# Moving the activation sums behind the next pair's additions, and three smaller moves, in a hybrid decoder layer

## The chip, the core and the metric

The kernel runs on one core of one Trainium2 chip. The metric is device time in microseconds from one execution of the whole program; lower is better. TensorE (PE) multiplies, VectorE (DVE), ScalarE (ACT) and GpSimd (POOL) do element-wise work, and SyncE (SP) as well as ACT issue DMA transfers. Each engine takes its own instructions strictly in the order in which they were built, and semaphores make it wait for others.

## What is computed

One layer of a decoder trunk on 1024 tokens of width 1024, in float32. Three branches read a normalised, projected x; then a ConvFFN is added.

```python
x += (sum_b sigmoid(G_b) * (branch_b @ W_br[b])) @ W_out     # RWKV-7, stick-breaking attention, memory attention
x += conv_ffn(x)

def memory_branch(q, mem, mem_g, w_kv, q_g, k_g):            # 256 memory tokens, 4 heads x 128
    kv = rms_norm(mem, mem_g) @ w_kv
    mk, mv = jnp.split(kv, 2, axis=-1)
    ...
def conv_ffn(x, g, w_up, conv_w, conv_b, w_down):            # D_FF = 2816
    h = rms_norm(x, g) @ w_up
    hp = jnp.pad(h, ((0, 0), (CONV_W - 1, 0), (0, 0)))
    acc = conv_b + hp[:, 0:t] * conv_w[0]
    for i in range(1, CONV_W):
        acc = acc + hp[:, i:i + t] * conv_w[i]
    gate, val = jnp.split(acc, 2, axis=-1)
    return (jax.nn.silu(gate) * val) @ w_down
```

## The kernel before

**Products.** A float32 product is made of three fast ones: each operand is split into a high part (a rounded copy, made by ACT) and a low part (the rest, made by DVE or POOL), and PE adds high x high, high x low and low x high. `split_w` does that for a weight: L83 makes `wh` on ACT, L86 or L89 makes `wl` on DVE or POOL.

**First half.** A long list of small items (projections, gates, key and query work, memory keys) is woven between the steps of the attention loops. Much of the order is left to a scheduler. Two helpers restrict it: `pinned` keeps an instruction in program order among those marked so, and `behind(ins, prev)` puts `ins` after `prev`. `last_fin` is the last copy of a finished PSUM bank that some item left behind. The attention of a head pair goes through `front` (L979, ACT), `weigh` (a scan on DVE, L985), `mid` (transposes on PE, copied by ACT at L997) and `back` (products of the tiles `at` with the values `A`). The keys of a head pair are split in `k_split` (L928, L929 on ACT, then L930, L931 on DVE). L936 copies a finished projection out of its bank, L937 squares it. The memory keys are made in `mk`, one head per call; L1119 and L1120 write the square and the scaled key of each head into two tiles `st["k"]`. Tiles come from `t4(tag)`: the tag names a ring of buffers, "w4" with 3 (the default) and "at" with 7. An instruction that takes a buffer waits for the last reader of what lay there, a DMA too.

**Up phase.** `up_phase` multiplies with W_up in blocks of two by two: seven products of 512-wide halves instead of eight, which needs sums of weights before and sums of activations behind. `pairs` lists 22 column pairs n = 0 to 21: even n are gate columns, odd n the value columns of the same block f = n // 2. `step(n, i)` issues product i of pair n; for n > 2 the order is 1, 5, 6, 2, 7, 4, 3. Each product is 12 matmuls. What DVE does with the banks: L1685 adds product 6's bank to `p1`, and the bank is then used again by product 7, which accumulates in it; L1698 and L1699 (behind product 7), L1708 (behind 4), L1717 (behind 3). `conv_half` makes the convolution of one half: L1627 on ACT, L1629 and L1630 on DVE; for even n a sigmoid `sg` on ACT (L1632); then the product of gate and value on DVE (L1635) into a tile `gall` (or `ga`, block 1). `prep1` to `prep3` make the next pair's weight sums on POOL (L1572, L1576, L1582, L1583) and split weights (L1554 on ACT, L1555 on POOL). `act_sums(f, late)` adds, when both halves of block f are there, the activation quarters (L1646, two additions for `late=False`, two for `late=True`) and stores them in DRAM (L1654, L1661, L1662, DMAs issued by ACT).

**Down phase.** `down_phase` goes through seven stages i of 11 blocks f. `prep` loads three blocks ahead and splits them: L1846 on DVE (some weights are differences), L1851 and L1852 on ACT, L1853 on DVE (`da`), L1854 on POOL (`dw`). At a stage's end `drain` takes the banks; `complete(tt)` then adds a finished output tile to the residual (L1874) in the next stage, `release` issues the stores. `last_residual` (L1915, L1916) adds the residual into `keep` late in stage 4.

Of the kernel before, what the change touches and what calls it, by code (L numbers as in the profile page):

```python
# [15 lines left out]
AF = mybir.ActivationFunctionType  # L16
# [34 lines left out]
class Trunk:  # L51
# [847 lines left out]
    def sb_qk(self, p, out):  # L899
        nc = self.nc  # L900
        st = {}
        lo64, hi64 = slice(0, 64), slice(64, 128)

        def k_fin(pp):
            kr, sq = self.t4(), self.t4()
            for h in range(2):
                self.leave(nc.scalar.activation(kr[:, h * 512 : (h + 1) * 512], pp[h], AF.Copy))
            nc.scalar.activation(sq, kr, AF.Square)
            st["k"] = sq, kr

        def k_ss():
            st["ex"] = self.expand_heads(self.head_norm(self.head_ss(st["k"][0]), 2, SBD, 1.0))

        def k_bc():
            kr = st["k"][1]
            bc = self.bcast_heads(st["ex"])
            for h in range(2):
                hs = slice(h * 512, (h + 1) * 512)
                nc.vector.scalar_tensor_tensor(kr[:, hs], kr[:, hs], self.par("sbk"), bc[h], ALU.mult, ALU.mult)
            st["K"] = [], []  # L920

        def k_split(i):
            kr = st["k"][1]
            K, KL = st["K"]
            for x in (K, KL):
                x.append(self.t4("qk", F32R))
            q, o = (lo64, hi64) if i == 0 else (hi64, lo64)
            nc.scalar.activation(K[i][q], kr[q], AF.Copy)  # L928
            nc.scalar.activation(K[i][o], kr[q], AF.Copy)  # L929
            nc.vector.tensor_tensor(KL[i][q], kr[q], K[i][q].bitcast(F32), ALU.subtract)  # L930
            nc.vector.tensor_tensor(KL[i][o], kr[q], K[i][q].bitcast(F32), ALU.subtract)  # L931

        def q_fin(pp):
            qr, sq = self.t4(), self.t4()
            for h in range(2):
                self.leave(nc.scalar.activation(qr[:, h * 512 : (h + 1) * 512], pp[h], AF.Copy))  # L936
            nc.scalar.activation(sq, qr, AF.Square)  # L937
            st["q"] = sq, qr

        def q_split(i):  # L940
            qr = st["q"][1]
            st.setdefault("S", []).append(self.t4("qk", F32R))
            S = st["S"][i]
            q, o = (lo64, hi64) if i == 0 else (hi64, lo64)
            g = self.par("sbq")[q]
            nc.scalar.activation(S[q], qr[q], AF.Copy, scale=g)
            nc.vector.scalar_tensor_tensor(S[o], qr[q], g, S[q].bitcast(F32), ALU.mult, ALU.subtract)
            if i == 1:
                out.extend((st["S"], *st["K"], st["f"]))

        def q_ss():
            nf = self.small("nf", [128, 16])
            st["f"] = self.head_norm(self.head_ss(st["q"][0]), 2, SBD, SBD ** -0.5, nf)

        w = self.I["w_in"]
        hooks = {1: lambda: k_split(1), 3: q_ss, 4: lambda: q_split(0), 6: lambda: q_split(1)}
        kq = {4: k_bc, 5: lambda: k_split(0)} if p else {5: k_bc, 6: lambda: k_split(0)}
        kh = {} if p else {k: functools.partial(self.difference, k - 3) for k in (3, 4, 5, 6)}
        return self.proj_item(w[18 + p], k_fin, kh), k_ss, self.proj_item(w[14 + p], q_fin, kq), hooks
# [82 lines left out]
    def mem_kv(self):  # L1042
        nc = self.nc
        mhi, mlo, sqs, st = [], [], [], {}
# [61 lines left out]
        def mk(h):  # L1106
            w = self.split_w(self.I["w_mk"][h])
            yield
            if h == 0:
                st["k"] = self.t4(), self.t4()  # L1110
            sq, kr = st["k"]
            hs = slice(h * 256, (h + 1) * 256)
            pk = self.ps("mm")[:, :256]
            for k in range(8):
                ks = slice(k * 128, (k + 1) * 128)
                self.mm3([pk], [a[:, ks] for a in w], [[mx(t, k, slice(0, 256))] for t in (mhi, mlo)], k == 0, k == 7)
                if k == 3:
                    yield
            nc.scalar.activation(sq[:, hs], pk, AF.Square)  # L1119
            nc.scalar.activation(kr[:, hs], pk, AF.Copy, scale=self.par("memk"))  # L1120
            self.mk = sq, kr, *st["r"]
            yield
# [394 lines left out]
    def up_phase(self, raws, t2, operand, high, low, late, sums):  # L1517
        nc = self.nc
# [19 lines left out]
        W, st = {}, {}  # L1538
# [125 lines left out]
        def step(n, i):  # L1664
# [15 lines left out]
            elif i == 6:  # L1680
# [2 lines left out]
                if (n, "u1") not in st:  # L1683
                    st[n, "u1"] = u_tile()
                self.pinned(nc.vector.tensor_tensor(st[n, "u1"][:, R2], Bk, st[n, "p1"], ALU.add))  # L1685
                if n > 2 and pairs[n - 1][2]:
                    act_sums(pairs[n - 1][1], True)
            elif i == 7:
                Bk = st.pop((n, "B"))
                product(n, 7, Bk, False, True)  # L1690
# [9 lines left out]
            elif i == 40:  # L1700
                Dk = st[n, "D"] = bank()
                product(n, 4, Dk, True, True)
            elif i in (4, 41):
                if i == 4:
                    step(n, 40)
                Dk = st.pop((n, "D"))
                v = st[n, "u2"]
                nc.vector.tensor_tensor(v[:, L2], v[:, L2], Dk, ALU.subtract)  # L1708
                if n == 0:
                    return st.pop((n, "u2"))  # L1710
                if n + 1 < len(pairs):
                    conv(n, 1, st.pop((n, "u2")))
            elif i == 3:
                C = st.pop((n, "C"))
                product(n, 3, C, False, True)
                u = st.pop((n, "u1"))
                nc.vector.tensor_tensor(u[:, R2], C, u[:, R2], ALU.add)  # L1717
                if n == 0:
                    return u
                if n + 1 == len(pairs):  # L1720
                    conv(n, 1, st.pop((n, "u2")))
                if n == 1:
                    return u
                conv(n, 0, u)
                if n + 1 == len(pairs):
                    self.last_sums = [functools.partial(act_sums, pairs[n][1], late) for late in (False, True)]
                elif pairs[n][2]:
                    act_sums(pairs[n][1], False)

        def u1_first(n):  # L1730
            A = st.pop((n, "A"))
# [48 lines left out]
        for n in range(1, len(pairs)):  # L1780
# [3 lines left out]
            for i in order:  # L1784
# [4 lines left out]
                if n == 1 and i == 4:  # L1789
                    step(2, 1)  # L1790
                elif n == 2 and i == 6:
                    conv(1, 0, u)
                elif n == 3 and i in (5, 6, 7, 4):
                    late, part = ((False, 0), (False, 1), (True, 0), (True, 1))[(5, 6, 7, 4).index(i)]
                    act_sums(0, late, (part,))
                if n == 1 and i == 6:
                    prep3(1)
                    prep1(2)
# [15 lines left out]
    def down_phase(self):  # L1814
        nc = self.nc
# [108 lines left out]
        for s, (i, f) in enumerate(steps):  # L1924
# [10 lines left out]
                t_sums(s // 2)  # L1935
            if s + ahead < len(steps):
                prep(s + ahead)
            if f < 4:
                complete(f)
            elif f == 5:  # L1940
                release()
            if s in (2, 4):
                self.last_sums.pop(0)()
# [184 lines left out]
```

## Time and profile before

| | us |
|---|---|
| median of 3 runs (lowest to highest) | 1789.28 (1788.69 to 1789.63) |
| profiled execution | 1788.33 |
| its span | 1786.6 |
| busy PE, DVE, ACT, POOL | 1774.7, 1185.1, 883.3, 698.3 |
| one up-phase pair (seven products) | 19.04 |

The granted clock was 1.000. In the views times are microseconds from the span's start; a timeline row has start, busy time, engine, line, operation, out<-in, shape and count, and in brackets the idle time ahead of it with what ended it. A group of equal neighbours stands in one row (x2, x3). In the list of waits a row reads: engine line waited for: us in total, times, longest. Lines are those of the kernel before; in the changed one, lines behind L1685 are two lower (four lower from L1727 to L1790).

### The profile page before, as it was taken

The numbers are of one execution on the slowest core, as the hardware profiler recorded it, in microseconds if no ns is written. First come the engines' busy times: TensorE is split into PE (matmuls) and PEld (weight loads), VectorE is DVE, ScalarE is ACT, GpSimd is POOL, SyncE is SP. The second block draws the span as 40 slices with busy tenths as digits, with TensorE's granted clock in tenths as the row PEclk, the third lists the DMA queues.
The fourth block names the chain that finished last, engine by engine and source line by source line (L and its number), as shares of the span: only waits on it lengthen the run. The fifth ranks groups of instructions, "written<-read, shape, count | busy, mean of one in ns | idle before, by whom it ended". The sixth has DMA issues, their size and how long they took to land.

```text
span 1786.6 us, 27452 instructions
## 1 busy us (share of the span) xinstructions
PE 1774.7 (99%) x10481; PEld 1442.4 (81%) x10481; DVE 1185.1 (66%) x1687; ACT 883.3 (49%) x1667; POOL 698.3 (39%) x409
## 2 busy tenths in 40 slices
PE   9999999999999999999999999999999999999999
PEld 7777778878888888787777888887888888888887
DVE  5666674787888655243533873698767777795597
ACT  6544344566566635444546434454444445445343
POOL 1233252222231012122433321257777677535454
PEclk9999999999999999999999999999999999999999
DMA  4256574111112333658763653323323333396475
GB/s 185 74 166 193 181 244 148 51 57 42 54 57 77 103 126 93 203 181 278 269 228 145 230 211 105 108 89 124 101 89 104 115 104 113 109 329 224 142 246 202
DMA packets 120757, 263.39 MB, mean 147 GB/s; under 512 B 28329, under 2 KB 41129, under 8 KB 120498
## 3 DMA queue, kind: packets, MB, share of 16 engines
q1 hardware_dynamic: 82434, 193.31, 33.1%
q10 hardware_dynamic: 34416, 55.72, 8.5%
q0 software_dynamic: 3776, 12.62, 2.3%
q8 instruction: 82, 1.34, 0.3%
q14 instruction: 49, 0.40, 0.1%
HBM read 180.04 MB, written 81.53 MB: 146 GB/s over the span
## 4 chain that ended last, share of the span: by engine, by line
PE 61%; issue 1%; DVE 1%; POOL 1%; ACT 1%; DMA 1%; ACTq 0%; DVEq 0%; POOLq 0%; SPq 0%
PE mm L139 53%; PE g L139 8%; PE g L122 1%; POOL dw L1854 1%; DMA vmd<-w 0%; ACT wh L83 0%; DMA qk<-vd 0%; DVE qk L715 0%; ACT w L885 0%; DVE gall L1646 0%; DVE w L886 0%; DVE ga L1635 0%; DVE keep L1874 0%; DVE g L1629 0%; DVE g L1630 0%
## 5 line engine op out<-in xcount | busy, mean ns | idle before, releaser
L89 POOL TENSOR_TENSOR wl<-wr,wh 128x1024 fp32r<-128x1024 f32 x58 | 147.8, 2550 | 368.2 <-ACT wh L83 355.0
L139 PE MATMUL mm<-xhi,wh 128*128 128x512 f32 x784 | 260.5, 413 | 1.4 <-ACT xhi L222 1.0
L139 PE MATMUL mm<-xlo,wh 128*128 128x512 f32 x784 | 243.6, 392 | 0.1
L139 PE MATMUL mm<-xhi,wl 128*128 128x512 f32 x784 | 242.2, 390 | 0.0
L139 PEld LDWEIGHTS mm<-xlo,wh 128*128 128x128 f32 x784 | 147.0, 188 | 33.4 <-DVE xlo L225 1.0
L139 PEld LDWEIGHTS mm<-xhi,wl 128*128 128x128 f32 x784 | 147.2, 188 | 32.7
L139 PEld LDWEIGHTS mm<-xhi,wh 128*128 128x128 f32 x784 | 136.6, 189 | 31.1 <-issue 7.9
L139 PE MATMUL mm<-dw,da 128*128 128x512 f32 x528 | 120.9, 390 | 0.0
L83 ACT ACTIVATE wh<-wr 128x1024 fp32r<-128x1024 f32 x75 | 79.5, 1060 | 81.5 <-PE mm L139 57.2
L139 PE MATMUL mm<-BT,l 128*128 128x512 f32 x504 | 117.9, 389 | 0.3 <-POOL l L1555 0.3
L139 PEld LDWEIGHTS mm<-dw,da 128*128 128x128 f32 x528 | 98.9, 188 | 21.3 <-DVE da L1853 0.8
L1854 POOL TENSOR_TENSOR dw<-draw,dw 128x512 fp32r<-128x512 f32 x55 | 83.6, 1530 | 76.1 <-ACT dw L1852 74.2
L985 DVE TENSOR_TENSOR_SCAN at<-at,at 128x128 f32<-128x128 f32 (+3 forms) x64 | 91.0, 1428 | 33.1 <-ACT at L979 33.0
L139 PEld LDWEIGHTS mm<-BT,l 128*128 128x128 f32 x504 | 94.5, 188 | 20.3 <-POOL l L1555 0.7
L139 PE MATMUL mm<-BT,wh 128*128 128x512 f32 x352 | 108.6, 390 | 1.7 <-DVE u L1685 1.7
L139 PE MATMUL mm<-B,wh 128*128 128x512 f32 x352 | 108.6, 389 | 0.0
L195 POOL TENSOR_TENSOR hf<-rs,half 128x16 f32<-128x16 f32 (+1 forms) x18 | 49.2, 2734 | 142.2 <-DVE rs L192 137.8
L1853 DVE TENSOR_TENSOR da<-draw,da 128x512 fp32r<-128x512 f32 x77 | 66.9, 877 | 49.1 <-ACT da L1851 48.8
L139 PE MATMUL g<-dw,da 128*128 128x512 f32 x396 | 90.6, 389 | 0.4 <-POOL dw L1854 0.4
L1851 ACT ACTIVATE da<-draw 128x512 fp32r<-128x512 f32 x77 | 48.3, 628 | 80.7 <-PE mm L139 29.9
L139 PEld LDWEIGHTS g<-dw,da 128*128 128x128 f32 x396 | 74.2, 188 | 16.2 <-POOL dw L1854 0.8
L1555 POOL TENSOR_TENSOR l<-it,l 128x1024 fp32r<-128x1024 f32 x20 | 48.0, 2402 | 85.5 <-ACT l L1554 85.5
(343 smaller groups left out, 3972.1 us busy)
## 6 DMA issues: line engine op xcount, KB each, us to landing
wr<-in_w_in_dram SPq DMA_DIRECT2D x49, 512.0 KB, 3.7
draw<-actd SPq DMA_DIRECT2D x77, 256.0 KB, 3.3
at<-scr SPq DMA_DIRECT2D x28, 512.0 KB, 5.6
draw<-in_w_down_dram SPq DMA_DIRECT2D x55, 256.0 KB, 4.8
rw<-in_w_up_dram SPq DMA_DIRECT2D x22, 512.0 KB, 3.6
actd<-gall ACTq DMA_DIRECT2D x41, 256.0 KB, 3.4
gsd<-w ACTq DMA_DIRECT2D x20, 512.0 KB, 2.7
wr<-in_w_up_dram SPq DMA_DIRECT2D x18, 512.0 KB, 3.6
```

The source lines that it names most:

```text
L83: ins = self.nc.scalar.activation(hi, raw, AF.Copy)
L89: self.last_wl = self.nc.gpsimd.tensor_tensor(lo, raw, hi.bitcast(F32), ALU.subtract)
L122: self.pinned(self.nc.tensor.transpose(out, in_, self.ident[:n, :n]))
L139: self.pinned(self.nc.tensor.matmul(*a, **k))
L195: nc.gpsimd.tensor_tensor(out, t[:, :n], self.half[:, :n], ALU.pow)
L985: self.pinned(nc.vector.tensor_tensor_scan(sn[:, :W][:, ::-1], sn[:, :W][:, ::-1], self.smask[:, 1024 - W :][:, ::-1], 1.0, ALU.mult, ALU. ...
L1555: self.last_low = keep(eng.tensor_tensor(lo, src, hi.bitcast(F32), ALU.subtract))
L1851: self.pinned(nc.scalar.activation(A[:, 0], a, AF.Copy))
L1853: self.pinned(nc.vector.tensor_tensor(A[:, 1], a, A[:, 0].bitcast(F32), ALU.subtract))
L1854: nc.gpsimd.tensor_tensor(Wt[:, 1], w, Wt[:, 0].bitcast(F32), ALU.subtract)
```

## The change

Four pieces.

1. In `k_split` both key copies on ACT are put behind `last_fin`.
2. The two memory-key tiles come from the ring "at" instead of "w4".
3. The activation sums of a block leave `step`. For odd pairs n - 1 > 2 they are now issued in pair n: the first two behind product 6's addition (L1685), the last two behind product 7's additions (L1699). Before, the first two stood at the end of pair n - 1, the last two behind L1685. Block 0's sums, spread over products 5, 6, 7 and 4 of pair 3, now stand at 5, 6, 6 and 7.
4. In stage 4 of the down phase the tiles are completed at blocks 0, 2, 4 and 6 instead of 0 to 3, and released at block 8 instead of 5.

```diff
@@ -925,8 +925,8 @@
             for x in (K, KL):
                 x.append(self.t4("qk", F32R))
             q, o = (lo64, hi64) if i == 0 else (hi64, lo64)
-            nc.scalar.activation(K[i][q], kr[q], AF.Copy)
-            nc.scalar.activation(K[i][o], kr[q], AF.Copy)
+            for x in (q, o):
+                self.behind(nc.scalar.activation(K[i][x], kr[q], AF.Copy), self.last_fin)
             nc.vector.tensor_tensor(KL[i][q], kr[q], K[i][q].bitcast(F32), ALU.subtract)
             nc.vector.tensor_tensor(KL[i][o], kr[q], K[i][q].bitcast(F32), ALU.subtract)
 
@@ -1107,7 +1107,7 @@
             w = self.split_w(self.I["w_mk"][h])
             yield
             if h == 0:
-                st["k"] = self.t4(), self.t4()
+                st["k"] = self.t4("at"), self.t4("at")
             sq, kr = st["k"]
             hs = slice(h * 256, (h + 1) * 256)
             pk = self.ps("mm")[:, :256]
@@ -1683,8 +1683,6 @@
                 if (n, "u1") not in st:
                     st[n, "u1"] = u_tile()
                 self.pinned(nc.vector.tensor_tensor(st[n, "u1"][:, R2], Bk, st[n, "p1"], ALU.add))
-                if n > 2 and pairs[n - 1][2]:
-                    act_sums(pairs[n - 1][1], True)
             elif i == 7:
                 Bk = st.pop((n, "B"))
                 product(n, 7, Bk, False, True)
@@ -1724,8 +1722,6 @@
                 conv(n, 0, u)
                 if n + 1 == len(pairs):
                     self.last_sums = [functools.partial(act_sums, pairs[n][1], late) for late in (False, True)]
-                elif pairs[n][2]:
-                    act_sums(pairs[n][1], False)
 
         def u1_first(n):
             A = st.pop((n, "A"))
@@ -1791,8 +1787,10 @@
                 elif n == 2 and i == 6:
                     conv(1, 0, u)
                 elif n == 3 and i in (5, 6, 7, 4):
-                    late, part = ((False, 0), (False, 1), (True, 0), (True, 1))[(5, 6, 7, 4).index(i)]
-                    act_sums(0, late, (part,))
+                    for late, part in {5: ((False, 0),), 6: ((False, 1), (True, 0)), 7: ((True, 1),)}.get(i, ()):
+                        act_sums(0, late, (part,))
+                elif n > 3 and n % 2 == 0 and i in (6, 7):
+                    act_sums(pairs[n - 1][1], i == 7)
                 if n == 1 and i == 6:
                     prep3(1)
                     prep1(2)
@@ -1935,9 +1933,11 @@
                 t_sums(s // 2)
             if s + ahead < len(steps):
                 prep(s + ahead)
-            if f < 4:
+            if i != 4 and f < 4:
                 complete(f)
-            elif f == 5:
+            elif i == 4 and f < 8 and f % 2 == 0:
+                complete(f // 2)
+            elif f == (8 if i == 4 else 5):
                 release()
             if s in (2, 4):
                 self.last_sums.pop(0)()
```

PE's order is the same in both. What moves elsewhere, at the places that the prediction speaks of:

ACT in head pair 1 of the attention, before. `qk_536` is the second split key tile of head pair 1, `w4_522` the projection that leaves its bank at L936, `at_534` a transposed attention tile that PE reads next.

```order
L928 ACTIVATE qk_536_3179<-w4_446_2750 64x1024
L979 ACTIVATE at_519_3114<-g_520_3115,nf_418_2590 128x512
L979 ACTIVATE at_519_3114<-g_521_3119,nf_418_2590 128x128
L929 ACTIVATE qk_536_3179<-w4_446_2750 64x1024
L936 ACTIVATE w4_522_3129<-mm_495_2977 128x512
L936 ACTIVATE w4_522_3129<-mm_496_2978 128x512
L83 ACTIVATE wh_527_3143<-wr_526_3141 128x1024
L937 ACTIVATE w4_523_3130<-w4_522_3129 128x1024
L997 ACTIVATE at_524_3134<-g_525_3135 128x384
L979 ACTIVATE at_531_3156<-g_532_3157,nf_418_2590 128x512
L979 ACTIVATE at_531_3156<-g_533_3161,nf_418_2590 128x256
L997 ACTIVATE at_534_3165<-g_535_3166 128x512
```

After:

```order
L979 ACTIVATE at_519_3114<-g_520_3115,nf_418_2590 128x512
L979 ACTIVATE at_519_3114<-g_521_3119,nf_418_2590 128x128
L936 ACTIVATE w4_522_3129<-mm_495_2977 128x512
L936 ACTIVATE w4_522_3129<-mm_496_2978 128x512
L83 ACTIVATE wh_527_3143<-wr_526_3141 128x1024
L937 ACTIVATE w4_523_3130<-w4_522_3129 128x1024
L997 ACTIVATE at_524_3134<-g_525_3135 128x384
L979 ACTIVATE at_531_3156<-g_532_3157,nf_418_2590 128x512
L979 ACTIVATE at_531_3156<-g_533_3161,nf_418_2590 128x256
L929 ACTIVATE qk_536_3179<-w4_446_2750 64x1024 x2
L997 ACTIVATE at_534_3165<-g_535_3166 128x512
L946 ACTIVATE qk_551_3264<-w4_522_3129,params_70 64x1024
```

The two copies of `qk_536` have gone from in front of the bank copies (L936) to the place between the second pair of L979 and the L997 that makes `at_534`.

POOL between pairs 3 and 4 of the up phase, before. `wl_1819` and `wl_1828` are low parts of pair 4's weights, `l4_1817` the low part of its weight sums, `it_1838` a sum for pair 5.

```order
L1555 TENSOR_TENSOR wl_1819_11338<-wr_1782_11128,wh_1818_11337 128x1024
L1555 TENSOR_TENSOR l4_1817_11321<-it_1815_11317,l4_1816_11320 128x1024
L1572 TENSOR_TENSOR it_1838_11476<-rw_1812_11294 128x512
L1576 TENSOR_TENSOR it_1838_11476<-it_1838_11476,rw_1811_11293 128x512
L1582 TENSOR_TENSOR rw_1812_11294<-rw_1811_11293,rw_1812_11294 128x512
L1555 TENSOR_TENSOR wl_1828_11417<-wr_1783_11129,wh_1827_11416 128x1024
```

After:

```order
L1555 TENSOR_TENSOR wl_1819_11339<-wr_1782_11128,wh_1818_11338 128x1024
L1555 TENSOR_TENSOR wl_1828_11412<-wr_1783_11129,wh_1827_11411 128x1024
L1555 TENSOR_TENSOR l4_1817_11322<-it_1815_11318,l4_1816_11321 128x1024
L1572 TENSOR_TENSOR it_1838_11472<-rw_1812_11294 128x512
L1576 TENSOR_TENSOR it_1838_11472<-it_1838_11472,rw_1811_11293 128x512
L1582 TENSOR_TENSOR rw_1812_11294<-rw_1811_11293,rw_1812_11294 128x512
```

The low part `wl_1828` has moved ahead of `l4_1817`, past the three sums.

DVE in pair 8 of the up phase, before; `u_1933` is written by L1685 and L1717, `u_1939` by L1698 to L1708.

```order
L1646 TENSOR_TENSOR gall_10748<-gall_10748 128x512 x2
L1618 MEMSET u_1933_12083 128x2
L1685 TENSOR_TENSOR u_1933_12083<-mm_1932_12070,p1_1928_12051 128x512
L1646 TENSOR_TENSOR gall_10748<-gall_10748 128x512 x2
L1618 MEMSET u_1939_12126 128x2
L1698 TENSOR_TENSOR u_1939_12126<-mm_1932_12070,p1_1928_12051 128x512
L1699 TENSOR_TENSOR u_1939_12126<-mm_1929_12053,u_1939_12126 128x512
L1708 TENSOR_TENSOR u_1939_12126<-u_1939_12126,mm_1940_12130 128x512
L1629 SCALAR_TENSOR_TENSOR g_1942_12145<-u_1939_12126,params_70,g_1942_12145 128x512
```

After (L1696, L1697, L1706 and L1715 are the old L1698, L1699, L1708 and L1717):

```order
L1618 MEMSET u_1933_12078 128x2
L1685 TENSOR_TENSOR u_1933_12078<-mm_1932_12065,p1_1928_12046 128x512
L1646 TENSOR_TENSOR gall_10748<-gall_10748 128x512 x2
L1618 MEMSET u_1939_12122 128x2
L1696 TENSOR_TENSOR u_1939_12122<-mm_1932_12065,p1_1928_12046 128x512
L1697 TENSOR_TENSOR u_1939_12122<-mm_1929_12048,u_1939_12122 128x512
L1646 TENSOR_TENSOR gall_10748<-gall_10748 128x512 x2
L1706 TENSOR_TENSOR u_1939_12122<-u_1939_12122,mm_1940_12130 128x512
L1715 TENSOR_TENSOR u_1933_12078<-mm_1929_12048,u_1933_12078 128x512
L1629 SCALAR_TENSOR_TENSOR g_1942_12145<-u_1939_12122,params_70,g_1942_12145 128x512
```

The two sums ahead of L1685 have gone behind it, the two behind it have gone behind the old L1699, and the old L1717 has come up ahead of the first L1629.

ACT at the end of pair 8 and the start of 9, before. `sg_1941` and `sg_1944` are the two sigmoid tiles, `l4_1960` the high part of pair 10's weight sums.

```order
L1627 ACTIVATE g_1942_12145<-u_1939_12126,params_70 128x512
L1627 ACTIVATE g_1943_12151<-u_1939_12126,params_70 128x512
L1627 ACTIVATE g_1945_12171<-u_1933_12083,params_70 128x512
L1554 ACTIVATE l4_1950_12190<-s4_1947_12183 128x512
L1632 ACTIVATE sg_1941_12144<-g_1942_12145 128x512
L1632 ACTIVATE sg_1941_12144<-g_1943_12151 128x512
L1669 ACTIVATE p1_1953_12207<-mm_1952_12194 128x512
L1627 ACTIVATE g_1946_12177<-u_1933_12083,params_70 128x512
L1632 ACTIVATE sg_1944_12170<-g_1945_12171 128x512
L1632 ACTIVATE sg_1944_12170<-g_1946_12177 128x512
L1554 ACTIVATE l4_1960_12245<-it_1959_12242 128x1024
```

After:

```order
L1627 ACTIVATE g_1942_12145<-u_1939_12122,params_70 128x512
L1627 ACTIVATE g_1943_12151<-u_1939_12122,params_70 128x512
L1627 ACTIVATE g_1945_12171<-u_1933_12078,params_70 128x512
L1627 ACTIVATE g_1946_12177<-u_1933_12078,params_70 128x512
L1554 ACTIVATE wh_1948_12186<-rw_1908_11916 128x1024
L1632 ACTIVATE sg_1941_12144<-g_1942_12145 128x512
L1632 ACTIVATE sg_1941_12144<-g_1943_12151 128x512
L1554 ACTIVATE l4_1950_12190<-s4_1947_12183 128x512
L1669 ACTIVATE p1_1953_12207<-mm_1952_12194 128x512
L1632 ACTIVATE sg_1944_12170<-g_1945_12171 128x512
L1554 ACTIVATE l4_1960_12245<-it_1959_12242 128x1024
L1632 ACTIVATE sg_1944_12170<-g_1946_12177 128x512
```

The second half's last sigmoid (from `g_1946`) now stands behind `l4_1960`; the copy of `wh_1948` has gone behind all four L1627.

## Prediction

> **What bounds the kernel now.** The page's part 1 comes first.
>
> ```profile
> PE 1774.7 (99%) x10481; PEld 1442.4 (81%) x10481; DVE 1185.1 (66%) x1687; ACT 883.3 (49%) x1667; POOL 698.3 (39%) x409
> ```
>
> TensorE is the bound: its 1774.7 us stand in a span of 1786.6, and the change leaves its instructions and their order alone. So the time can only move by stretches in which PE waits. The list of PE's waits has ten rows; these are the ones that the change can touch (total, times, longest, in us).
>
> ```profile
> PE mm L139 <- DVE u L1685: 1.7, 1, 1.7
> PE mm L139 <- DVE wl L86: 0.9, 2, 0.5
> PE mm L139 <- ACT w L936: 0.4, 1, 0.4
> PE g L139 <- POOL dw L1854: 0.4, 1, 0.4
> PE mm L139 <- POOL l L1555: 0.3, 1, 0.3
> ```
>
> Together they are 3.7 us, all single events. By the timeline around them PE also loses about 0.1 us after each while its pipeline refills. So at most some 4.2 us can be gained. What can be lost has no such cap, since the up phase runs the same pair of column blocks 22 times: a wait that the new order makes there comes back in each.
>
> **Key copies (sb_qk).** ACT's timeline in head pair 1, then PE's.
>
> ```profile
> 366.08 1.06 ACT L929 ACTIVATE qk<-w 64x1024 fp32r<-64x1024 f32 x1
> 367.04 1.05 ACT L936 ACTIVATE w<-mm 128x512 f32<-128x512 f32 x2
> ...
> 370.40 1.04 ACT L979 ACTIVATE at<-g,nf 128x512 f32<-128x512 f32 x2
> 371.33 0.60 ACT L997 ACTIVATE at<-g 128x512 f32<-128x512 f32 x1
> ```
>
> ```profile
> 367.67 0.50 PE L139 MATMUL mm<-xhi,wh 128*128 128x512 f32 x1 [0.42 <-ACT w L936]
> 372.93 1.09 PE L139 MATMUL mm<-at,A 128*64 128x128 f32 x14
> ```
>
> PE waits at 367.67 because a key copy (L929) runs ahead of the bank copies (L936). With both key copies behind, L936 starts about 0.5 us earlier (when PE has left the bank) and some 0.1 of the 0.42 stays: gain 0.3 and the refill, 0.4 in all. But the copies don't vanish. The built order puts them between the second L979 and the L997 at 371.33, and ACT runs from 367.04 on without a gap. That L997 then moves by -0.5 + 2 x 0.97 (1.06 less the overlap of neighbours) to about 372.75, ends near 373.35, and PE wants its tile from about 372.55 on (372.93 less the 0.4 gained). The first of the 14 matmuls reads an older tile. New wait 0.7, refill 0.1: the part loses 0.4. Ends: -0.5 (no matmul of the group needs the tile early) to +0.6. Head pairs 0, 2 and 3 already stood in the new order.
>
> **Memory keys (mem_kv).** ACT's timeline, then one PE row.
>
> ```profile
> 620.97 0.47 ACT L1120 ACTIVATE w<-mm,params 128x256 f32<-128x256 f32 x1 [2.44 <-DMA vmd<-w]
> 621.34 1.05 ACT L83 ACTIVATE wh<-wr 128x1024 fp32r<-128x1024 f32 x1
> 622.42 1.24 ACT L1020 ACTIVATE ys<-mm,jk 64x128 f32<-64x128 f32 x4
> ```
>
> ```profile
> 627.32 0.39 PE L139 MATMUL mm<-qk,wl 128*128 128x256 f32 x1 [0.49 <-DVE wl L86]
> ```
>
> L1120 waits 2.44 us for the store of the memory values, whose buffer it takes; the weight's high part (L83) stands behind it, and both wl waits (0.9) follow. In buffers of "at" this wait is gone. The first PE wait goes whole. At the second, the chain is 1.0 us earlier (it now waits for the L1020 copies, whose bank PE has just left) while PE wants it 0.5 earlier: 0.3 stays. Gain 1.0 with the refills; ends 0.5 and 1.2. The two "at" buffers taken are long read; nothing queues for them.
>
> **Sums at the start (pairs 3 and 4).** Rows of DVE, ACT, POOL and PE.
>
> ```profile
> 1216.25 1.77 DVE L1646 TENSOR_TENSOR gall<-gall 128x512 f32<-128x512 f32 x1
> 1238.91 0.68 DVE L1685 TENSOR_TENSOR u<-mm,p 128x512 f32<-128x512 f32 x1
> ```
>
> ```profile
> 1218.18 1.06 ACT L1554 ACTIVATE wh<-wr 128x1024 fp32r<-128x1024 f32 x1 [2.08 <-PE mm L139]
> ```
>
> ```profile
> 1219.32 2.41 POOL L1555 TENSOR_TENSOR wl<-wr,wh 128x1024 fp32r<-128x1024 f32 x1
> 1227.49 2.41 POOL L1555 TENSOR_TENSOR l<-it,l 128x1024 fp32r<-128x1024 f32 x1 [5.76 <-ACT l L1554]
> 1240.08 2.84 POOL L1555 TENSOR_TENSOR wl<-rw,wh 128x1024 fp32r<-128x1024 f32 x1
> ```
>
> ```profile
> 1229.96 5.28 PE L139 MATMUL mm<-BT,l 128*128 128x512 f32 x22 [0.30 <-POOL l L1555]
> ```
>
> In pair 4, L1685 at 1238.91 stood behind two sums of pair 3's block; all four sums now stand inside pair 3, and the 1.7 goes: gain 1.8. The 0.30 at 1229.96 grows. In the new POOL order pair 4's second wl stands ahead of the l<-it that PE waits for, and it comes too late for that: ACT's first wh (1218.18 before) now follows the store of the third sum, which comes right behind the one at 1216.25 and ends near 1219.65, and a bank copy (0.6): it starts near 1220.5, its wl runs 1221.65 to 1224.05; the fourth sum meets it and ends 0.55 later; the fourth's store and then the second wh follow at 1225.0 to 1226.1; its wl to 1228.5; l<-it to 1230.9 instead of 1229.9. Loss 1.0; ends 0 and 1.4.
>
> **Sums in every even pair, 6 to 18.** Rows of pair 8 and the start of 9: DVE, ACT, POOL, PE.
>
> ```profile
> 1314.77 4.27 DVE L1646 TENSOR_TENSOR gall<-gall 128x512 f32<-128x512 f32 x2
> 1319.69 0.69 DVE L1699 TENSOR_TENSOR u<-mm,u 128x512 f32<-128x512 f32 x1
> 1321.58 0.69 DVE L1708 TENSOR_TENSOR u<-u,mm 128x512 f32<-128x512 f32 x1 [1.20 <-PE mm L139]
> 1323.17 1.46 DVE L1629 SCALAR_TENSOR_TENSOR g<-u,params,g 128x512 f32<-128x512 f32 x2 [0.90 <-ACT g L1627]
> 1330.54 1.30 DVE L1635 TENSOR_TENSOR gall<-g,sg 128x512 f32<-128x512 f32 x2
> 1332.46 0.69 DVE L1685 TENSOR_TENSOR u<-mm,p 128x512 f32<-128x512 f32 x1 [0.62 <-PE mm L139]
> ```
>
> ```profile
> 1329.91 1.20 ACT L1632 ACTIVATE sg<-g 128x512 f32<-128x512 f32 x2 [1.62 <-DVE g L1630]
> 1332.30 1.06 ACT L1554 ACTIVATE l<-it 128x1024 fp32r<-128x1024 f32 x1 [1.18 <-PE mm L139]
> ```
>
> ```profile
> 1316.88 1.62 POOL L1572 TENSOR_TENSOR it<-wr 128x512 f32<-128x512 f32 x1
> ...
> 1320.16 1.28 POOL L1582 TENSOR_TENSOR wr<-wr,wr 128x512 f32<-128x512 f32 x1
> 1321.40 4.76 POOL L1555 TENSOR_TENSOR wl<-rw,wh 128x1024 fp32r<-128x1024 f32 x2
> ```
>
> ```profile
> 1334.98 0.62 PE L139 MATMUL mm<-BT,wh 128*128 128x512 f32 x2
> ```
>
> L1685 of pair 9 must leave its bank before product 7 goes on in it at 1334.98; before, it ended at 1333.15 and had 1.8 us. An L1646 that meets a POOL operation ends 0.54 after it (the two at 1314.77 end at 1319.04, POOL's at 1318.50), and POOL's next one is drawn out by about 0.4 (2.84 against 2.41). The new order has the first two sums at 1314.77 (4.27 as before, the others' place) and the last two behind L1699, where 1.2 us of idle time stand. There the third is asked for at 1320.3, when L1582 has just begun (1320.16): it ends at 1321.44 + 0.55 = 1322.0; the fourth waits for the drawn-out wl, to 1324.25, and ends at 1324.8. L1708 follows at 1324.7, 3.1 later than before. From the first L1629 the chain to the last L1630 takes 1330.48 - 1323.17 = 7.3, one L1717 fewer and one L1635 more: it ends at 1333.6. The last sg (0.60), which the new ACT order has behind l<-it, ends at 1334.2, its L1635 (0.65 pitch) and L1685 (0.68) at 1335.55, and 0.05 later PE goes on: 0.6 late, with refill 0.65. Seven pairs: 4.5.
>
> The Trainium skill (SBUF — State Buffer, "Who interferes with whom") says that a DVE instruction with two SBUF inputs and a GpSimd instruction that reads SBUF exclude each other for a whole instruction. The rows agree on who blocks, yet not on the remainder: taken literally a blocked sum would need its full 0.68 after POOL's end, 0.13 more than the 0.55 above, and two of them in seven pairs would make the loss 6.3 instead of 4.5.
>
> In pair 4 no POOL operation meets the last sums, but the last sg still waits for l<-it: 1332.30 + 0.97 + 0.60 + 0.65 + 0.68, with signal times 1335.3, is 0.3 after 1334.98: loss 0.4. Pair 20 has other work around it and enough room: 0.
>
> **Down stage 4.**
>
> ```profile
> 1750.57 5.78 DVE L1916 TENSOR_TENSOR keep<-keep 128x512 f32<-128x512 f32 x4
> 1756.27 0.68 DVE L1853 TENSOR_TENSOR da<-draw,da 128x512 fp32r<-128x512 f32 x1
> ```
>
> ```profile
> 1752.70 30.08 PE L139 MATMUL mm<-dw,da 128*128 128x512 f32 x132
> ```
>
> Spread additions let the weight of block 7 through: the 0.4 goes, gain 0.5. What is late next is the da at 1756.27. It ends at 1756.95 and PE wants it at 1752.70 + 26 x 0.227 = 1758.6, or 1758.1 without the old wait: 1.2 of room, on a DVE that has no gap in these rows. Each row there costs 1.1 more when POOL is in its way (the 1.77 at 1216.25 against 0.68 here), and additions that now stand among the last blocks' rows meet POOL more often. None more: 0; three more: 2.1. I take two: 2.2 - 1.2 = 1.0. The part loses 0.5 (ends -0.5 and +1.6).
>
> **Sum.** +0.4 - 1.0 - 1.8 + 1.0 + 4.5 + 0.4 + 0.5 = +4.0. On the profiled execution's 1788.33 that is 1792.3; it lies 0.95 below the median, 1789.28, so I forecast 1793.3. A measurement of this kernel tells 0.2% (3.6 us) from no change.
>
> **Rivals.** (A) Not slower: the third sum gets ahead of L1582. It asks only 0.15 us after it; if it wins, both last sums are over by 1321.7, L1708 stays in place, and only sg behind l<-it costs, 0.4 in each of seven pairs: 2.8 for 4.5, with the down stage at its lower half about +1.8, 1791.1. For: the gap is small. Against: both times hang on the same PE product, so the order should be the same in all pairs. (B) The change does what it says: no wait appears in the pairs, nor in head pair 1, the start and the down stage: -0.4 - 1.0 - 1.8 - 0.5 = -3.7, 1785.6. It needs 0.6 us of room that I don't see in any pair. (C) More of the same: 0.9 per pair (the literal rule's length, or ACT late for the first sg), 6.3, and 1.6 in the down stage: +6.9, 1796.2.
>
> **Numbers.** Forecast 0.60, two thirds of it above the 3.6 (terms may move 1 us together); A 0.17; B 0.07; C 0.16. Slower 0.40 + 0.16, rounded with A's upper end to 0.57; faster 0.07; same 0.36. The range leaves out B and the top of C: 1788.8 to 1796.2.
>
> **What would show it.** Right: the list of PE's waits has DVE u L1685 seven or eight times at 0.3 to 0.7, a first L997 wait near 373, POOL l L1555 at over 1 us; the rows at 1239, 620.97 and 1742 are gone. Wrong: fewer than four L1685 waits, or L1632 ahead of the l<-it in time in the even pairs; or a POOL L1582 that starts behind the third sum.

## The result

The changed kernel took 1797.11 us (median of 5 runs, 1796.46 to 1799.03), the kernel before, timed beside it, 1789.28: ratio 1.0045, interval 1.0030 to 1.0059. It is slower, by 7.8 us where 4.0 were forecast, and it lies 0.9 above the top of the range. Timed once more together with the experiments it gave 1796.24 against 1789.48, ratio 1.0040 (1.0027 to 1.0054). The profiled execution took 1796.46, with a span of 1794.7 and a granted clock of 1.000 as before. The page's part 1 of the changed kernel:

```profile
PE 1779.2 (99%) x10481; PEld 1442.4 (80%) x10481; DVE 1198.0 (67%) x1687; ACT 879.8 (49%) x1667; POOL 699.3 (39%) x409
```

No engine has more to do: DVE's instructions are as many as before (1687), and their 13 us more are time in which they stood blocked, most of all the sums (L1646, 40 of one form: 70.1 us in all instead of 53.8). The list of PE's waits of the changed kernel, the rows that are new or stand in place of one shown before:

```profile
PE mm L139 <- DVE u L1618: 4.0, 7, 0.6
PE mm L139 <- POOL l L1555: 1.5, 1, 1.5
...
PE mm L139 <- DVE da L1851: 0.9, 1, 0.9
PE mm L139 <- ACT at L997: 0.7, 1, 0.7
...
PE mm L139 <- DVE xlo L225: 0.5, 1, 0.5
...
PE mm L139 <- DVE wl L86: 0.2, 1, 0.2
```

The 1.7 for L1685, the 0.4 for L936 and the 0.4 for the weight of the down phase are gone, the wait for wl fell from 0.9 to 0.2. In their place come a wait that occurs seven times, one of 1.5, and two single ones (0.9 and 0.7). The row of xlo is new too, but it lies in the start of the kernel, which the change leaves alone. The seven are put down to L1618, a 0.06 us memset that stands right behind L1685 and ended 0.01 after it. Product 7 goes on in the bank that L1685 reads, so L1685 is the instruction that PE waits for, as the rows of pair 8 below show.

What a wait costs is more than its idle time. The windows view of the same 229 us of the up phase, before and then after (PE's busy time and matmuls come first behind the width):

```profile
1297.00:1526.00 229.00, 229.00 (x1012) 189.63 (x1011) 168.87 (x252) 106.72 (x145) 166.64 (x97) 1.00 0.32 104
```

```profile
1297.00:1526.00 229.00, 225.56 (x989) 184.81 (x988) 179.23 (x246) 100.17 (x139) 163.06 (x94) 1.00 0.32 103
```

Six of the seven waits lie in it. PE is idle for 3.44 us, 0.57 for each, but it does 23 matmuls fewer: at 229 / 1012 = 0.226 us each that is 5.2 us, 0.87 for each. DVE's busy time rises by 10.4 in the same stretch, with fewer instructions. The groups by form say which ones (min/median/max in ns), before and then after:

```profile
L1646 DVE TENSOR_TENSOR gall<-gall x40: 678/694/2879, 1215.0 to 1589.5; 128x512 f32<-128x512 f32 x40
```

```profile
L1646 DVE TENSOR_TENSOR gall<-gall x40: 677/1631/2884, 1216.5 to 1596.9; 128x512 f32<-128x512 f32 x40
```

About half of these sums ran unblocked before (median 694); now most are blocked (1631).

**The steps, place by place.** PE runs the same 10481 matmuls in the same order in both kernels, so the n-th of one can be laid beside the n-th of the other, and the difference of their starts grows by each delay at its place. In us, after the forecast the changed kernel's first profile and the profile of its repetition:

| place | forecast | first | again |
|---|---|---|---|
| key copies (367 to 373) | +0.4 | +0.54 | +0.49 |
| memory keys (623, 627) | -1.0 | -0.89 | -0.94 |
| pair 4, wait for L1685 (1239) | -1.8 | -1.95 | -1.96 |
| pair 4, l<-it (1229) | +1.0 | +1.18 | +1.18 |
| pairs 7 to 19, seven waits | +4.5 | +6.15 | +6.16 |
| pair 5 (1258) | +0.4 | +0.35 | +0.36 |
| pairs 20 and 21 (1550, 1563) | 0 | +0.12 | +0.40 |
| down stage (1741, 1758) | +0.5 | +0.79 | +0.87 |
| elsewhere | 0 | +1.8 | +1.1 |
| end | +4.0 | +8.13 | +7.68 |

### The profile page after: what moved, and what is told of

Its sections match the earlier page's. It is cut to its first block, busy times and chain, and to the rows that moved or that the text cites. A ratio compares the mean times of both kernels' runs of the same rounds, so it can differ in the third digit from the quotient of the medians.

```text
span 1794.7 us, 27443 instructions
## 1 busy us (share of the span) xinstructions
PE 1779.2 (99%) x10481; PEld 1442.4 (80%) x10481; DVE 1198.0 (67%) x1687; ACT 879.8 (49%) x1667; POOL 699.3 (39%) x409
## 3 DMA queue, kind: packets, MB, share of 16 engines
q8 instruction: 82, 1.34, 0.3%
## 4 chain that ended last, share of the span: by engine, by line
PE 49%; DVE 7%; issue 4%; ACT 4%; POOL 2%; DMA 2%; ACTq 0%; SPq 0%; DVEq 0%; POOLq 0%
PE mm L139 41%; PE g L139 7%; DVE gall L1646 1%; POOL dw L1852 1%; ACT g L1627 1%; PE g L122 1%; DVE gall L1635 1%; ACT sg L1632 1%; DVE at L1359 1%; DVE g L1630 1%; DVE mg L1366 0%; DMA w<-mrd 0%; ACT wh L1554 0%; DVE qk L715 0%; DMA wr<-in_w_out_dram 0%
## 5 line engine op out<-in xcount | busy, mean ns | idle before, releaser
L1627 ACT ACTIVATE g<-u,params 128x512 f32<-128x512 f32 x88 | 64.9, 770 | 68.8 <-DVE u L1706 63.7
```

What stands on the lines that cost most here:

```text
L1627: keep(nc.scalar.activation(c, u[:, 2 + h * 512 : 514 + h * 512], AF.Identity, scale=self.par("cw2", m), bias=self.par("cb", m)))
```

## Pair 8 of the changed kernel

The timelines of DVE, POOL, ACT and PE. Up to here PE is 2.0 us later than before.

```profile
1322.19 4.44 DVE L1646 TENSOR_TENSOR gall<-gall 128x512 f32<-128x512 f32 x2
1326.56 0.68 DVE L1706 TENSOR_TENSOR u<-u,mm 128x512 f32<-128x512 f32 x1
1328.09 1.46 DVE L1629 SCALAR_TENSOR_TENSOR g<-u,params,g 128x512 f32<-128x512 f32 x2 [0.25 <-ACT g L1627]
...
1330.77 0.75 DVE L1629 SCALAR_TENSOR_TENSOR g<-u,params,g 128x512 f32<-128x512 f32 x1
1331.66 1.29 DVE L1635 TENSOR_TENSOR gall<-g,sg 128x512 f32<-128x512 f32 x2
...
1334.95 0.74 DVE L1630 SCALAR_TENSOR_TENSOR g<-u,params,g 128x512 f32<-128x512 f32 x1
1336.36 0.69 DVE L1635 TENSOR_TENSOR gall<-g,sg 128x512 f32<-128x512 f32 x1 [0.67 <-ACT sg L1632]
1336.98 0.68 DVE L1685 TENSOR_TENSOR u<-mm,p 128x512 f32<-128x512 f32 x1
```

```profile
1321.98 1.30 POOL L1582 TENSOR_TENSOR wr<-wr,wr 128x512 f32<-128x512 f32 x1
1323.23 2.85 POOL L1555 TENSOR_TENSOR wl<-rw,wh 128x1024 fp32r<-128x1024 f32 x1
```

```profile
1330.11 1.05 ACT L1554 ACTIVATE wh<-rw 128x1024 fp32r<-128x1024 f32 x1
1331.06 1.06 ACT L1632 ACTIVATE sg<-g 128x512 f32<-128x512 f32 x2
...
1334.29 1.06 ACT L1554 ACTIVATE l<-it 128x1024 fp32r<-128x1024 f32 x1
1335.73 0.60 ACT L1632 ACTIVATE sg<-g 128x512 f32<-128x512 f32 x1 [0.37 <-DVE g L1630]
```

```profile
1336.75 0.39 PE L139 MATMUL mm<-B,wl 128*128 128x512 f32 x1
1337.71 0.73 PE L139 MATMUL mm<-BT,wh 128*128 128x512 f32 x2 [0.57 <-DVE u L1618]
```

The third sum is asked for 0.2 after L1582 has begun, the fourth meets wl; together they take 4.44 where two unblocked ones take 1.3. They end at 1326.63, 0.55 after POOL's wl (1326.08). L1706 (old 1708) starts at 1326.56, 3.0 later than before once the 2.0 are taken off, and everything behind follows: the last L1630, the last sg, L1635, L1685, and PE 0.05 after it. The matmul that waited starts 0.96 after its neighbour instead of 0.23 (0.74 more), the next one loses 0.11, the few behind it 0.02: 0.87. The seven pairs lose 0.86 to 0.92 each, 6.15 together. The last sg stands behind l<-it on ACT, yet it waited for DVE's L1630, not for l<-it, which was over at 1335.35. One small wait for ACT is in the chain: the first sg stands behind wh, its first half ends at 1331.66, and DVE, free at 1331.52, starts L1635 then.

## Experiments

**The four parts, each alone.** The diff is the hunk of that name; the rest is the kernel before.

> The kernel before with only the key copies behind the bank copies. My theory (parts add up, each is a trade of one PE wait for another): the wait at 367.67 (0.42) goes, a new wait of PE for ACT L997 of about 0.7 appears near 373, net +0.3 to +0.6 us, 1789.6 to 1789.9. Rival (the mid-kernel loss of about 1.3 us between 594 and 1057 that the changed kernel shows comes from this part, because DVE's order after the key copies is shifted): +1.6 to +2.0 us and steps in PE's times near 594, 1033 and 1056 as in the changed kernel. Second rival (those steps are scatter of one execution): no step there.

> The kernel before with only the memory keys in the other buffers. My theory: both waits of PE for DVE wl L86 shrink from 0.9 together to 0.2 or 0.3, -0.9 to -1.0 us, about 1788.3. Rival (the keys' longer stay in the ring of attention tiles delays work near 594, 1033 and 1056, the unexplained +1.3 us of the changed kernel): net +0.3 us or so, with steps at those places.

> The kernel before with only the activation sums moved (all of pairs 3 to 20). My theory: this part carries nearly the whole loss: +1.2 at pair 4's l<-it, -1.95 at pair 4's L1685, +0.35 in pair 5, 7 x 0.85 = +6.0 in the odd pairs 7 to 19, +0.4 in pair 21, -0.3 near 1550: +5.7 us, 1795.0. Rival (the losses of the parts feed on each other, the pairs' wait being as long as it is only with the other parts in): 7 x 0.65 as predicted and 0 in pair 21, +3.7 us, 1793.0.

> The kernel before with only the spread additions in down stage 4. My theory: the wait at 1741.88 goes (-0.6), the da of block 2 in the last stage comes late behind the four residual additions (+1.2 to +1.4): net +0.7 us, 1790.0. Rival (that da is late in the changed kernel only since the up phase left ACT, DMA queues or DVE later): only the gain, -0.6 us, 1788.7.

Against 1789.55 for the kernel before beside them:

| part alone | us | ratio, interval |
|---|---|---|
| 1, key copies | 1790.16 | 1.0003 (0.9994 to 1.0011) |
| 2, memory keys | 1788.38 | 0.9993 (0.9984 to 1.0002) |
| 3, sums | 1795.71 | 1.0032 (1.0020 to 1.0043) |
| 4, down stage | 1790.69 | 1.0006 (0.9998 to 1.0015) |

Only part 3 can be told from no change; its profile has the seven steps of pairs 7 to 19, and +1.18, -1.96 and +0.36, as in the whole. The differences, +0.6, -1.2, +6.2 and +1.1, make 6.7: the whole (6.8 to 7.8) is the sum of its parts within what these medians can tell.

Part 1 in the timelines of ACT and PE (here of the whole change; alone it is the same, 0.7 for L997):

```profile
370.25 1.06 ACT L979 ACTIVATE at<-g,nf 128x512 f32<-128x512 f32 x2
371.33 2.14 ACT L929 ACTIVATE qk<-w 64x1024 fp32r<-64x1024 f32 x2
373.38 0.57 ACT L997 ACTIVATE at<-g 128x512 f32<-128x512 f32 x1
```

```profile
372.92 0.43 PE L139 MATMUL mm<-at,A 128*64 128x128 f32 x2
374.01 1.09 PE L139 MATMUL mm<-at,A 128*64 128x128 f32 x12 [0.66 <-ACT at L997]
```

L997 stands behind both copies, and PE needs it at the third of the 14 matmuls. Part 2 does what it should: L1120 no longer waits for a store, and its weight's copy follows at once.

```profile
619.83 0.47 ACT L1120 ACTIVATE at<-mm,params 128x256 f32<-128x256 f32 x1
620.18 1.06 ACT L83 ACTIVATE wh<-wr 128x1024 fp32r<-128x1024 f32 x1
```

**Leave the last two sums out.** Part 3 alone, but from pair 6 on the third and fourth sum aren't computed.

```diff
-                tt(sa[:, 3], a12, sa[:, 1], ALU.subtract)
+                skip or tt(sa[:, 3], a12, sa[:, 1], ALU.subtract)
```

> The sums moved as in the changed kernel (this part alone), but from pair 6 on the third and fourth sum are not computed (what is stored for them is stale); the first two sums and all stores stand. My theory (those two sums, held by POOL, make the chain late): no waits in the odd pairs 7 to 19, L1706 near its old time: 1789.55 + 1.2 - 1.95 + 0.35 to +0.6, 1789.1 to 1789.4. Rival (the first two sums behind L1685, which draw out POOL's operations, make the chain late): at least half of the 6.0 us stays, 1792 or more.

1788.68 against 1790.13 beside it, ratio 0.9992 (0.9983 to 1.0001). Its timeline of DVE in pair 8:

```profile
1320.06 0.69 DVE L1697 TENSOR_TENSOR u<-mm,u 128x512 f32<-128x512 f32 x1
1322.05 0.69 DVE L1706 TENSOR_TENSOR u<-u,mm 128x512 f32<-128x512 f32 x1 [1.30 <-PE mm L139]
```

L1706 waits for PE again, as before the change, and no wait for L1685 is left in any odd pair from 7 on. The two sums there are what brings the seven steps. Without them, and in the dose run below, the scheduler's order goes back too (L1715 behind an L1635, wh ahead of the L1627 on ACT), so these two runs alone don't part the sums from that order. In the changed kernel's rows above, though, the first L1629 waits for ACT and not for L1715, and wh costs no more than the 0.14.

**The sigmoid's place.** Part 3 alone, with the l<-it of the even pairs from 6 on put behind the last sg on ACT, where it stood before.

```diff
+            self.behind(ins, after)
...
+            w = hl(..., after=self.last_sg if n > 5 and n % 2 == 0 else None)
```

> The sums moved as in the changed kernel (this part alone), and in pairs 5 to 19 the high part l<-it is put behind the last sigmoid sg, as it stood before. My theory (the third and fourth sums meet POOL's L1582 and wl, L1706 is 3 us late, and the chain to the last L1630 carries that on; the place of sg does not matter): the seven waits of 0.57 stay, each costing 0.85, only pair 5's 0.35 goes, so 1795.2 to 1795.7. Rival (sg behind l<-it makes the waits): all waits in the odd pairs go, 1789.55 + 1.2 - 1.95 = 1788.8.

1795.83, ratio 1.0033 (1.0020 to 1.0046): no better than part 3. Its list of PE's waits (the eighth is pair 21's), and a row of ACT in pair 8 (L1634 and L1632 are the lines 1632 and 1630 of the other kernels):

```profile
PE mm L139 <- DVE u L1620: 4.7, 8, 0.7
```

```profile
1335.18 0.60 ACT L1634 ACTIVATE sg<-g 128x512 f32<-128x512 f32 x1 [1.42 <-DVE g L1632]
```

Free of l<-it, the last sg stands idle for 1.42 and waits for DVE. So in the late pairs ACT's order is not what is late. The wait in pair 5 is gone, though: there, where no POOL operation stretches the sums, the order on ACT was the cause, as forecast.

**Dose: one blocked sum instead of two.** Part 3 alone, the third sum with the first two.

```diff
+                    if n > 5 and i == 6:
+                        act_sums(pairs[n - 1][1], False)
+                    act_sums(pairs[n - 1][1], i == 7 or n > 5, (i - 6,) if n > 5 else (0, 1))
```

> Part 3 alone, but from pair 6 on the third sum stands with the first two behind L1685, and only the fourth is left behind L1699. Dose theory: the even pairs lose time because two sums there meet GpSimd, one after the other (4.4 us for the two, against 1.3 unblocked), and L1706 moves by 3 us, where only about 2.5 of room are. With three behind L1685 (the third falls into the gap of GpSimd between 1318.5 and 1320.2) one blocked sum is left behind L1699: it takes at most 1.75, L1706 is at most 0.9 us late and the chain to the last L1630 regains at least 1.5 us. So no DVE u wait in pairs 7 to 19, and the seven times 0.85 go: 5.9 below part 3 alone, ratio about 0.9995 (1789). Rival (any sum behind L1699 costs, by what stands in the order and not by its length): at least half of the waits stay, 0.4 us or more each, ratio 1.0015 or more. Pair 4's and pair 5's waits stay in both.

1790.13 against 1789.75, ratio 1.0001 (0.9992 to 1.0010). Its timelines of DVE and POOL in pair 8:

```profile
1314.12 5.18 DVE L1646 TENSOR_TENSOR gall<-gall 128x512 f32<-128x512 f32 x3
...
1320.57 1.69 DVE L1646 TENSOR_TENSOR gall<-gall 128x512 f32<-128x512 f32 x1
1322.18 0.68 DVE L1706 TENSOR_TENSOR u<-u,mm 128x512 f32<-128x512 f32 x1
```

```profile
1320.43 1.28 POOL L1582 TENSOR_TENSOR wr<-wr,wr 128x512 f32<-128x512 f32 x1
```

A sum behind L1697 (old 1699) still collides (1.69 instead of 0.68), but L1706 is now only about 0.5 late, and none of the seven waits is left. One collision is nearly free here, and the second exceeds the room. It isn't quite free: PE's starts slip by 0.09 more in each of the seven even pairs, 0.6 in all, in steps too small to show as idle time. That takes back the 0.4 that the moves in pairs 4 and 5 gain on balance, so that the run shows no gain, where about 1789 was expected; what PE waits for there was not traced.

**Pair 4 alone.** The kernel before, with only the second block's sums moved inside pair 4 and pair 6's l<-it behind the last sg of pair 4.

```diff
+                if n > 2 and pairs[n - 1][2] and n != 4:
...
+                elif n == 4 and i in (6, 7):
+                    act_sums(1, i == 7)
```

> The kernel before with the sums of one block only moved, that of pair 3, which stand behind L1685 and L1699 of pair 4; block 0's sums stay spread over products 5, 6, 7 and 4 of pair 3, all later blocks stay as they were, and pair 6's l<-it is put behind pair 4's last sigmoid. My theory (POOL does nothing while pair 4's third and fourth sums run, so nothing is late): pair 4's wait of 1.69 goes at no cost, -1.9 us, 1787.6. Rival (pair 5 waits 0.35 all the same, or pair 4's l<-it wait grows to 1.5 as in the changed kernel): -1.5 or -0.7.

1788.06 against 1790.13, ratio 0.9990 (0.9981 to 0.9998). Its steps are -1.96 at 1239 and none at 1229 or 1258. In these runs the l<-it at 1229 is late only when block 0's sums move too.

**The down stage.** Part 4 with the four residual additions (L1916) moved out of stage 4 into blocks 4 to 7 of stage 2.

```diff
-            if (i, f) == (4, 9):
-                last_residual()
+            if i == 2 and 4 <= f < 8:
+                last_residual((f - 4,))
```

> The kernel before with the additions of down stage 4 spread as in the changed kernel, and the four residual additions (with their loads) moved from the end of stage 4 into blocks 4 to 7 of the last stage. My theory (the late da of block 2 stands behind those four additions, each held by POOL): no wait near 1758 and none at 1741.88, -0.6 us, 1788.9. Rival (da is late because its own load or ACT's copy is late): the wait near 1758 stays, about 1790.6 as with the spread alone.

1788.37 against 1790.13, ratio 0.9991 (0.9982 to 1.0000); -0.63 at 1741 stays and no new wait follows. What it takes away, in the changed kernel's timelines of DVE and PE:

```profile
1758.15 0.69 DVE L1851 TENSOR_TENSOR da<-draw,da 128x512 fp32r<-128x512 f32 x1 [1.40 <-ACT da L1849]
1758.76 6.90 DVE L1914 TENSOR_TENSOR keep<-keep 128x512 f32<-128x512 f32 x4
1765.58 0.68 DVE L1851 TENSOR_TENSOR da<-draw,da 128x512 fp32r<-128x512 f32 x1
```

```profile
1766.32 3.96 PE L139 MATMUL mm<-dw,da 128*128 128x512 f32 x15 [0.90 <-DVE da L1851]
```

The residual additions (L1914, old 1916) took 6.90 instead of 5.78. They also started later: with PE's shift of 6.7 there taken off, 1758.76 is 1.5 behind the 1750.57 of before, for the da ahead of them waited 1.40 for ACT's copy. So the da behind them came late, and PE waited 0.9. But part 1 alone, which leaves the down phase as it was, shows nearly the same wait; the list of its PE waits and its timeline of DVE:

```profile
PE mm L139 <- DVE da L1853: 0.8, 1, 0.8
```

```profile
1753.29 6.87 DVE L1916 TENSOR_TENSOR keep<-keep 128x512 f32<-128x512 f32 x4
```

With its shift of 1.2 taken off, these additions too start 1.5 later than in the profile of before; ahead of them ACT spent 2.40 on issuing two stores (L1871, 1743.45) instead of 1.34 (1742.12), with the copies of da behind that. One key copy alone has a wait of 0.8 there as well. So it is a race, in which ACT's order of work and POOL's operations both have a share, and it needs no part 4 to be lost; the profiled execution of before had won it. Part 4 alone had a wait of 1.4 there: it may make the margin smaller, and how much can't be told from single profiles.

**One key copy.** Only the second copy behind the bank copies.

```diff
-            nc.scalar.activation(K[i][o], kr[q], AF.Copy)
+            self.behind(nc.scalar.activation(K[i][o], kr[q], AF.Copy), self.last_fin)
```

> Only the second key copy (L929's other half) goes behind the bank copies of head pair 1, the first stays where it was. Theory (ACT's queue is full from 367 on, so that two moved copies delay the L997 that PE wants at 372.6, by 0.7): one copy moved is one copy of delay, 0.97 less 0.5 gained, the L997 ends near 372.4 and no wait follows; at 367 PE's wait for L936 falls from 0.42 to 0.1 or less. The steps: -0.5 at 367, 0 at 372 to 373, so -0.5 in all, a time that cannot be told from the kernel before. Rival (the L997 wait comes with any copy behind the bank copies): 0.2 us or more at 372 to 373 and no gain.

1789.23 against 1789.75, ratio 0.9997 (0.9988 to 1.0006), which tells nothing by itself; the timeline of ACT does:

```profile
370.82 1.06 ACT L929 ACTIVATE qk<-w 64x1024 fp32r<-64x1024 f32 x1
371.78 0.57 ACT L997 ACTIVATE at<-g 128x512 f32<-128x512 f32 x1
```

L997 ends at 372.35 and PE's 14 matmuls start at 372.43 without a wait: -0.53 at 367 and nothing given back. The whole 0.42 went, not three quarters of it.

**What helped, together.** Part 2, one key copy, pair 4 alone, part 4 with the residual additions moved.

> What the single runs showed as gains, put together, without the sums of the even pairs from 6 on: the memory keys in other buffers (-1.0), one key copy behind (-0.5), the sums of the first block alone moved inside pair 3, with the l<-it of pair 6 behind the last sg of pair 4 (-1.95), the down stage's additions spread and the four residual additions put into the last stage's earlier blocks (-0.6). Theory (the gains lie at different places of PE and add): -4.0, 1785.5, ratio 0.9977. Rival (the places share slack, so that what is gained at one is waited for at the next): less than half of it, ratio 0.999 or more.

1784.43 (1784.10 to 1785.04) against 1789.75, ratio 0.9968 (0.9956 to 0.9981): 5.3 us below the kernel before and 12 below the changed one. The profiles differ by 3.9: the four steps make about 4.1, and 0.3 is lost in the start, which no part edits. Its list of PE's waits has only seven rows, none of them over 0.3 among those that the change touched:

```profile
PE mm L139 <- POOL l L1557: 0.3, 1, 0.3
PE mm L139 <- DVE wl L86: 0.2, 1, 0.2
```

**The changed kernel again.**

> The whole change once more, for what the terms leave over: its profile showed 1.8 us outside every edited place (0.5 in the start, 0.3 near 594, 1.0 between 1033 and 1057), and the parts' medians sum to 1.1 less than the whole. Theory (scatter between executions, for the single parts showed 0 to 0.5 there): the edited places give the same steps again, within 0.1 each (7 times 0.85, +1.2, -1.95, +0.35, +0.5 at 372, -0.9 at 623), while 1033 to 1057 gives at most 0.35; median about 1796.5. Rival (the parts together make a delay between 1033 and 1057 that no part makes alone): 0.8 or more there again.

1796.24. The steps stand in the table above: the edited places repeat within 0.1, except pair 21 (0.39, then 0.67), and 1033 to 1057 fell from 1.0 to 0.14. The rival falls: that microsecond was scatter of one execution.

## Why the prediction came out as it did

**Right: the direction, and the mechanisms.** PE's work stayed the same, the gains were single and the loss recurred. With 2.0 us taken off for the shift, the working of pair 8 reads beside the measured rows: L1706 at 1324.7 against 1324.6, the first L1629 at 1326.3 against 1326.1, the last L1630 done at 1333.6 against 1333.7, L1685 done at 1335.55 against 1335.7, PE going on at 1335.6 against 1335.7. That the two late sums start this chain was shown by leaving them out, by the dose and by the sigmoid's place, which changes nothing in these pairs. The terms for the key copies, the memory keys, pair 4 and pair 5 are within 0.2.

**Rival A** (the third sum gets ahead of L1582) did not occur: it came 0.2 behind, in all seven pairs. **Rival B** needed room that wasn't there. **Rival C** has the size that was measured, 0.88 per pair where it put 0.9, and hardly for the reasons it gave, so that its size is largely luck. By the prediction's literal reading of the Trainium skill (SBUF — State Buffer, "Who interferes with whom") the blocked sum would end 0.68 after GpSimd's operation; the trace has 0.55 again (1326.63 against 1326.08), as the working took it. Rival C's other reason, ACT late for the first sg, is worth 0.14 in pair 8, as shown above.

**Wrong: the size of the term for the seven pairs.** The step is "0.6 late, with refill 0.65. Seven pairs: 4.5." It measured 0.74 late, and 0.13 of refill: 0.87 in pair 8, 6.15 in the seven. Two small errors add up. The prediction took 0.05 for the refill, although its opening part had read about 0.1 behind each wait off the timeline; that is 0.08 per pair. And PE went on 0.1 later than the rows added up to (0.74 for 0.62, which was rounded down to 0.6): the stretch from the first L1629 to the last L1630 began 0.2 earlier and took 7.6 instead of 7.3, 0.14 of it the wait for the first sg. A tenth weighs little in 20 us but much in a difference of 0.6, and this term counts it seven times. It makes 1.65 of the 2.3 (first profile) or 2.6 (second) by which the named terms were too small.

**Wrong, smaller:** "Pair 20 has other work around it and enough room: 0" holds for pair 20 and not for what it leaves late: pair 21 waits (0.39 and 0.67), for a gain of 0.27 at 1550. Pair 4's l<-it (+1.18 for +1.0), the key copies and the down stage (+0.8 for +0.5) each came out 0.1 to 0.4 dearer. In the down stage the working was another than the measured one: it put two rows of 1.1 behind POOL, and one such row (1.1) came together with additions that started 1.5 late.

**What no term names.** With the measured sizes (6.3 and 6.6 in the two profiles, 6.4 between them) the prediction's own sum gives 1788.33 + 6.4 + 0.95 = 1795.7. The repetition is 0.5 above it, the first measurement 1.4. A step of 0.29 near 594 stands in all three profiles with both key copies behind and in none of the ten others; what links it to them was not traced. In the start, which no kernel edits, PE lost 0.3 to 0.56 at 9.4 in eight of the 13 other profiles and not in that of before, whose execution lay 0.95 below its median: there as in the down stage's race it was a lucky one. The rest stays open, within the scatter of the medians.

## What to carry to other kernels

When a saturated engine waits rarely, a move can only gain single waits, but a move inside a repeated loop pays its mistake each time around: lay the chain of one turn out to 0.1 us, and let the range grow with the count. A collision costs little until it exceeds the room, so look for the smallest part of a move that still brings the gain: here the sums of one pair instead of all, one key copy instead of two. A wait in one profile of a race says little; look at the same place in profiles of kernels that leave it alone.

## What the runs showed of the hardware

A listed wait of PE understates its cost. The idle time counts from the modelled end of the last matmul (0.39 long) though the next could have started 0.23 after its start, and the start behind the wait's end is followed by one that comes another 0.11 late: 0.57 listed cost 0.86 to 0.92 in each of seven places, and 1.7 listed at 1239 gave 1.96 back.

A two-input DVE addition that met a GpSimd one ended 0.55 us after it, in the changed kernel (1326.63 and 1326.08) as with one sum alone (1322.26 and 1321.71), and GpSimd's next wl took 2.85 in place of 2.41. Two in a row thus cost 4.44 in place of 1.3, most of it waiting.
